# Four pieces of the residual's transposition moved into the norm of the second MLP, and the last modulation vectors streamed through four other buffers

## The chip, the cores and the metric

The kernel runs on one core of a Trainium2 chip. The core has engines that work side by side: TensorE (PE in the profile, with its weight loads as PEld) multiplies matrices, VectorE (DVE) and ScalarE (ACT) work element by element, GpSimd (POOL) does small things, and SyncE (SP) issues the transfers from memory. The metric is the time of one execution on the device in microseconds; lower is better.

## The reference

The reference is a decoder trunk of two layers over 256 positions of 2048 channels. Each layer has a token mixer (a convolution module in layer 0, a Mamba-2 mixer in layer 1) and an MLP with a squared ReLU. Each is preceded by an RMS norm whose result is scaled and shifted by vectors that come from a conditioning vector `c`, and its output is gated by a third such vector and added to the residual `h`:

```python
sc = jax.nn.silu(c)
for i in range(DEPTH):
    mod = (sc @ w_mod[i] + b_mod[i])[:, None, :]
    sh1, sc1, g1, sh2, sc2, g2 = jnp.split(mod, 6, axis=-1)
    ...
    h = h + g1 * mix
    u = rmsnorm(h, norm_mlp_g[i]) * (1 + sc2) + sh2
    h = h + g2 * sq_relu_mlp(u, mlp_w1[i], mlp_w2[i])
return rmsnorm(h, final_norm_g)
```

All is float32. The widths that matter here: `w1` is 2048 x 8192 and `w2` 8192 x 2048; the Mamba mixer's output matrix `wout` is 4096 x 2048.

## The kernel before

**Layout.** The residual is kept as four tiles `h[0]` to `h[3]`, channels on the 128 partitions, four groups of 128 channels and 256 positions to a tile. Weights stream from memory in tiles of 1 MB (`w32`, three buffers, `load_w`). Each tile is split in two halves, and each half in a high part `wh` (a cast on ScalarE, L387) and a low part `wl` (a subtraction on VectorE, L389); both have three buffers. TensorE multiplies the parts and adds up in banks of its accumulator memory. There are eight banks: six of the pool `mm` for the large products and two of the pool `ms` for small ones.

**Order.** The program is traced from top to bottom. A planner then gives every engine a fixed order: what comes first in the program goes first when it is ready, and `high_priority(n)` moves an instruction's rank forward. `issue_after(x)` ties an instruction behind `x` on its engine. Buffers with one tag rotate; a new user waits until the old one's readers are done. Transfers of `stream` (L371) keep the program's order in SyncE's queue.

**Small steps.** Some work is written as generators in `todo`. `block`, the routine for one 512-column block of a matrix, calls `step` (L486) after every second group of products, and each step runs one generator to its next `yield`. `lag(n)` is `n` empty steps.

**Vectors.** The modulation vectors are computed from `w_mod` by `gemv` (L294): a 1 MB piece is fetched (`fetch`, L277) and multiplied with `silu(c)` on VectorE (L317), with the sum over the columns taken along. `pump` starts them in between the products, at rates such as `RATE_OUT` (24 over the 32 tiles of `wout`) and `RATE_LAST` (8 over the twelve tiles of the opening of the second MLP). The attribute `rings` names the tags whose buffers the pieces go to: `("wm",)` in all of layer 1, that is two buffers. The tag `hid` has four buffers of the same size; in the Mamba mixer they hold `out_hl[:4]`, what the first half of `wout` multiplies, and in the MLP the hidden activations.

**Where the change lies.** `mamba` ends with `wout`: four blocks of its first half, then four of its second half (`into_h` adds the gated result to `h`; the very last block is of the kind `single`, L402). Then `mlp(1, ...)` (L1042):

1. It loads the first tile of `w1` and calls `rstd_bcast` (L544). This sums the squares over the channels with TensorE (L575), takes root and reciprocal (L581, L582), forms a diagonal (L549) and broadcasts it with one more product (L554). While the small engines work, `turn` (L285) keeps TensorE occupied with products of constants (`turn_over`, L558): three ahead of the broadcast (`AFTER_SUMS`) and four behind it (`TO_FIRST`, called by `outer`).
2. `outer` (L494) multiplies the first three column blocks of `w1` together, with two `mm` banks for each. For every quarter `g` of the channels `make(g)` (L1054) first scales and shifts that quarter into `u` (`modulate`, L605, with its cast L538), and then three tiles are multiplied.
3. `act` (L1063) squares the positive results and stores them in `hid`.
4. `to_rows` (L1101) is put into `todo`. The second MLP accumulates with positions on the partitions, so the residual is transposed: for each tile `h[b]` and each half `q` of the positions four transposes go to one `ms` bank (L1110), and ScalarE copies the bank into `ht[q]` (L1111), which sits in the two `wm` buffers. Two empty steps follow each of these eight pieces. After that it spreads the gate `G2` along rows by products (L1120, L1124, L1126) and loads the final norm's factor.
5. The last column block of the first quarter of `w1` runs through `block`, then `w2` through `block_t` (L451), and so on for the other quarters.

Of the kernel before, what the change touches and what calls it, by code (L numbers as in the profile page):

```python
# [15 lines left out]
P = 128  # L16
T = 256
D = 2048
# [5 lines left out]
Q = 128  # L24
# [159 lines left out]
def lag(n):  # L184

    for _ in range(n):
        yield


class Trunk:  # L190
    def __init__(self, ctx, nc, tc, a):
        self.nc, self.tc, self.a = nc, tc, a
        pool = lambda n, **kw: ctx.enter_context(tc.tile_pool(name=n, **kw))
        self.one = pool("one", bufs=1)
        self.big = pool("big", bufs=1)
        self.wp = pool("wp", bufs=1)
        self.tp = pool("tp", bufs=2)
        self.mm = pool("mm", bufs=6, space=PSUM)
        self.ms = pool("ms", bufs=2, space=PSUM)
        self.dr = pool("dr", bufs=1, space=DRAM)  # L200
        self.uid = 0
        self.jobs = []
        self.todo = []
        self.ahead = AHEAD
        self.ring, self.rings = 0, ("wm", "hid", "hid")
        self.mod = {}
        self.rows_left = []
        self.held = []
        self.spare = 1
        self.act = None  # L210
        self.side = self.mm, "mm"
        self.prologue()
# [72 lines left out]
    def turn(self, out, n):  # L285

        if self.held:
            key, w = self.held.pop(0)
            with self.tc.issue_after(self.pe):
                self.gemv(*key, w=w)  # L290
        else:
            self.pe = self.turn_over(out, n, self.pe)

    def gemv(self, layer, seg, ct, parts=((0, 4),), w=None):  # L294

        nc = self.nc
        w = self.fetch(layer, seg, ct) if w is None else w
        g, i = divmod(ct, 4)
        m = self.mod_tile(layer, seg, g)
        if (layer, seg, g) in PE_GROUPS:  # L300

            if i == 0:
                while len(self.rows_left) > self.spare:
                    self.columns()
                self.row_sums = self.bank(*self.side)
            for t in range(4):
                kt = 4 * i + t
                self.pe = nc.tensor.matmul(
                    self.row_sums[32 * t:32 * t + 32, :], lhsT=self.scol[:, kt:kt + 1].broadcast_to([P, 32]),
                    rhs=w[:, t * 512:(t + 1) * 512], start=i == 0, stop=i == 3, skip_group_check=True).ins  # L310
            if i == 3:
                row = self.t("t2", [P, 512], bufs=3)
                with self.tc.issue_after(self.act):
                    nc.scalar.copy(out=row, in_=self.row_sums)
                self.rows_left.append([self.row_sums, row, m, layer, seg, g, 0])
            return
        self.sum = nc.vector.scalar_tensor_tensor(out=w, in0=w, scalar=1.0, in1=self.scb, op0=ALU.mult,  # L317
                                                  op1=ALU.mult, accum_out=m[:, i:i + 1]).ins
        for i0, i1 in parts:
            if i + 1 == i1:  # L320
                self.mod_done(layer, seg, g, i0, i1)
# [720 lines left out]
    def mlp(self, layer, ss, pump=None, after=None, first=None):  # L1042
        nc, a = self.nc, self.a
        w = self.load_w(a["w1"][layer, 0][0])
        with self.tc.high_priority(AHEAD_CHAIN):
            half = self.split_half(w, 0, None, self.evac)
            r = self.rstd_bcast(ss, D)
        u = []
        st = {"acc": [None] * 4, "ss": []}
        gate = lambda b: self.mod_tile(layer, G2, b)  # L1050
        self.sq_row = self.t("mom", [P, 2, 4], bufs=1)
        self.part = [None] * 2

        def make(g):  # L1054
            self.need(layer, SC2, SH2, kg=g)
            with self.tc.high_priority(0 if g else AHEAD_CHAIN):
                u.append(self.modulate(r, layer, SC2, SH2, g))
            return u[g]

        for c in range(4):  # L1060
            hid = [None] * 4

            def act(b, j, parts):  # L1063
                if hid[b] is None:
                    self.rings = ("wm",)
                    hid[b] = self.b("hid", [P, 4, 2 * T], F32R)
                s = self.total(parts)
                q = self.t("a", [P, T], bufs=3)
                if len(parts) == 1:
                    nc.scalar.activation(out=q, in_=s, func=AF.Relu)  # L1070
                    s = q
                    nc.vector.tensor_mul(q, q, q)
                else:
                    nc.vector.scalar_tensor_tensor(out=q, in0=s, scalar=0.0, in1=s, op0=ALU.max, op1=ALU.mult)
                self.split_x(hid[b], j, q)

            if c == 0:
                self.outer([a["w1"][layer, b] for b in range(OPEN)], make, act, first or (lambda g: 0),
                           there=[(w, [half])], hi_after=self.sq)
                if layer == 1:  # L1080
                    self.todo.append(self.to_rows())
            for b in range(0 if c else OPEN, 4):
                self.block(a["w1"][layer, 4 * c + b], u, lambda j, parts, b=b: act(b, j, parts), pump=pump)
            if layer == 1:
                for b in range(4):
                    self.block_t(a["w2"][layer, c, b], hid, self.into_rows(b, c == 3), by_half=c == 3 and b == 3)
                continue
            for b in range(4):
                if c == 3:
                    self.need(layer, G2)  # L1090
                if b < 3:
                    ev = self.into_h(st, b, gate, after, acc=False) if c == 3 else None
                    self.block_t(a["w2"][layer, c, b], hid, self.into_turned(st, b, c, ev), pump=pump)
                    continue
                ev = self.into_h(st, b, gate, after) if c == 3 else self.into_acc(st, b, c == 0)
                self.block(a["w2"][layer, c, b], hid, ev, pump=pump, single=c == 3)
        assert not self.todo
        return st["ss"]


    def to_rows(self):  # L1101

        nc = self.nc
        self.need(1, G2)
        self.ht = [self.b("wm", [P, D], bufs=2) for _ in range(2)]
        for b in range(4):
            for q in range(2):
                ps = self.bank(self.ms, "ms")
                for j in range(4):
                    nc.tensor.transpose(ps[:, j * P:(j + 1) * P], self.h[b][:, j, q * Q:(q + 1) * Q], self.ident)  # L1110
                nc.scalar.copy(out=self.ht[q][:, b * 512:(b + 1) * 512], in_=ps)  # L1111
                yield from lag(2)
        self.gate_row, self.fg_row = [], []
        for i in range(2):
            v = self.b("h", [P, 2, 512])
            for k in range(2):
                ps = self.bank(self.ms, "ms")
                m = self.mod_tile(1, G2, 2 * i + k)
                dg = self.t("t2", [P, 4, P], bufs=3)
                nc.vector.tensor_tensor(  # L1120
                    out=dg, in0=self.ident.rearrange("p (o k) -> p o k", o=1).broadcast_to([P, 4, P]),
                    in1=m.rearrange("p (j o) -> p j o", o=1).broadcast_to([P, 4, P]), op=ALU.mult)
                yield from lag(3)
                nc.tensor.matmul(ps, lhsT=self.ones, rhs=dg.rearrange("p j k -> p (j k)"), start=True, stop=True)  # L1124
                yield
                nc.scalar.copy(out=v[:, k, :], in_=ps)  # L1126
                self.gate_row.append(v[:, k, :])
        for i in range(2):
            v = self.b("h", [P, 2, 512])
            src = self.a["fg"][:, i * 1024:(i + 1) * 1024]  # L1130
            nc.scalar.dma_start(out=v.rearrange("p k n -> p (k n)"), in_=src.broadcast_to([P, 1024]))
            self.fg_row += [v[:, 0, :], v[:, 1, :]]
# [39 lines left out]
    def mamba(self, ss):  # L1172
        nc, a = self.nc, self.a
# [74 lines left out]
        while self.todo:  # L1248
            self.step()
        self.need(1, G1)  # L1250
        for b in range(4):
            self.block(a["wout"][1, b], self.out_hl[4:], self.into_h(st, b, gate), pump=pump, single=b == 3)
        self.need(1, SC2, SH2)
# [236 lines left out]
```

## Time and profile before

| | us |
|---|---|
| median of 3 runs | 2538.79 |
| lowest and highest of the runs | 2536.79, 2539.12 |
| the profiled execution | 2537.33 |
| its span (first to last recorded instruction) | 2535.5 |
| mean granted clock of TensorE | 0.999 of full speed |
| norm of the second MLP (last product of `wout` to first product of `w1`) | from 1807.6 to 1812.4 |
| transposes of the residual, 32 instructions in all | from 1810.1 to 1905.9 |
| ScalarE's copies of the transposed residual, 8 | 0.587 each |

How to read it: the page gives the busy time of each engine as a share of the span, and a chain of work that is followed back from the last instruction, so that the engine which set the end has the largest share of it. A row of the timeline has the start, the time it took, the engine, the line and what was written from what, and in brackets the idle time before it with what ended it. `x4` means that four records were merged. Products of float32 operands that are not marked for the fast float32 form appear as two records.

### The profile page before, as it was taken

What the parts mean: (1) busy time and instruction counts of PE and PEld (TensorE: products, weight loads), DVE (VectorE), ACT (ScalarE), POOL (GpSimd) and SP (SyncE); (2) the same over time, 40 slices, a digit from 0 to 9 for tenths busy, and PEclk for the clock granted to TensorE, in tenths of its full rate; (3) what the DMA queues carried; (4) which work ended last, traced back from release to release, by engine and by line L of the source; (5) the groups of instructions that cost most, each with busy time, mean ns of one, the idle gap of its engine ahead of it and who ended that gap; (6) DMA issues with size and microseconds to landing.
All of it is one profiled execution on the core that took longest, in us unless ns stands there. A gap on an engine that the chain in (4) does not pass through costs nothing.

```text
span 2535.5 us, 36834 instructions
## 1 busy us (share of the span) xinstructions
PE 2509.7 (99%) x14596; PEld 2166.1 (85%) x14596; DVE 1937.3 (76%) x2524; ACT 1320.2 (52%) x2026; POOL 145.1 (6%) x201
## 2 busy tenths in 40 slices
PE   9999999999999999999999999999999999999998
PEld 7788799988888888888888888888998888888887
DVE  6799888878878888888787878998875565565565
ACT  2088654544434435457777777744454443443444
POOL 0011000000100000001000000000001101001000
PEclk9999999999999999999999999999999999999999
DMA  9998898788888878856555555688765555555554
GB/s 401 420 351 286 343 347 312 281 332 316 321 309 334 322 307 336 311 201 229 199 190 179 171 189 189 254 322 318 288 249 196 194 188 193 189 190 192 193 189 149
DMA packets 94894, 664.31 MB, mean 262 GB/s; under 512 B 10977, under 2 KB 11105, under 8 KB 16769
## 3 DMA queue, kind: packets, MB, share of 16 engines
q1 hardware_dynamic: 89138, 643.82, 68.6%
q0 software_dynamic: 5152, 16.97, 2.4%
q8 instruction: 114, 1.87, 0.3%
q10 hardware_dynamic: 432, 1.19, 0.1%
q14 instruction: 58, 0.48, 0.0%
HBM read 656.50 MB, written 2.20 MB: 260 GB/s over the span
## 4 chain that ended last, share of the span: by engine, by line
PE 89%; DVE 5%; DMA 3%; ACT 2%; issue 1%; SPq 0%; POOL 0%; DVEq 0%; ACTq 0%; POOLq 0%
PE mm L418 49%; PE mm L402 11%; PE mm L460 8%; PE mm L462 8%; PE mm L461 8%; DMA hid<-wmT 2%; DVE taps L693 2%; ACT taps L675 1%; PE mm L797 1%; DVE hid L317 1%; PE ms L1413 1%; DMA wm<-wmT 1%; DVE wm L317 1%; PE ms L797 0%; DVE taps L687 0%
## 5 line engine op out<-in xcount | busy, mean ns | idle before, releaser
L389 DVE TENSOR_TENSOR wl<-w,wh 128x1024 fp32r<-128x1024 f32 x768 | 940.2, 1229 | 474.1 <-ACT wh L387 469.4
L387 ACT CAST wh<-w 128x1024 fp32r<-128x1024 f32 x768 | 806.4, 1051 | 932.2 <-PE mm L418 480.6
L418 PE MATMUL mm<-u,wh 128*128 128x512 f32 x3136 | 994.6, 398 | 0.0
L418 PEld LDWEIGHTS mm<-u,wl 128*128 128x128 f32 x3136 | 587.9, 188 | 139.9 <-DVE wl L389 1.9
L418 PE MATMUL mm<-u,wl 128*128 128x256 f32 x3136 | 617.3, 278 | 1.4 <-DVE wl L389 1.4
L418 PEld LDWEIGHTS mm<-u,wh 128*128 128x128 f32 x3136 | 479.4, 189 | 7.2 <-issue 4.9
L460 PE MATMUL mm<-wh,hid 128*128 128x512 f32 x896 | 350.7, 391 | 0.0
L462 PE MATMUL mm<-wh,hid 128*128 128x512 f32 x896 | 348.7, 389 | 0.0
L461 PE MATMUL mm<-wl,hid 128*128 128x512 f32 x896 | 348.6, 389 | 0.0
L317 DVE SCALAR_TENSOR_TENSOR wm<-wm,scb 128x2048 f32<-128x2048 f32 x134 | 306.2, 2285 | 13.8 <-DMA wm<-wmT 13.7
L402 PE MATMUL mm<-u,wh 128*128 128x256 f32 x1408 | 253.7, 284 | 0.5 <-ACT u L538 0.3
L402 PEld LDWEIGHTS mm<-u,wh 128*128 128x128 f32 x1408 | 218.3, 192 | 3.5 <-ACT u L538 1.3
L461 PEld LDWEIGHTS mm<-wl,hid 128*128 128x128 f32 x896 | 168.2, 188 | 35.5 <-issue 0.5
L462 PEld LDWEIGHTS mm<-wh,hid 128*128 128x128 f32 x896 | 168.2, 188 | 35.4
L460 PEld LDWEIGHTS mm<-wh,hid 128*128 128x128 f32 x896 | 168.2, 188 | 35.1 <-issue 1.0
L402 PE MATMUL mm<-u,wl 128*128 128x256 f32 x704 | 196.1, 283 | 0.3 <-DVE wl L389 0.2
L418 PE MATMUL mm<-hid,wh 128*128 128x512 f32 x448 | 142.0, 398 | 0.0
L402 PEld LDWEIGHTS mm<-u,wl 128*128 128x128 f32 x704 | 133.7, 192 | 0.7 <-DVE wl L389 0.7
L317 DVE SCALAR_TENSOR_TENSOR hid<-hid,scb 128x2048 f32<-128x2048 f32 x46 | 105.2, 2287 | 20.5 <-DMA hid<-wmT 19.8
L675 ACT ACTIVATE taps<-u,par 128x256 f32<-128x256 f32 x248 | 102.4, 500 | 9.1 <-DVE u L665 5.3
L418 PEld LDWEIGHTS mm<-hid,wl 128*128 128x128 f32 x448 | 84.1, 188 | 19.7
L346 POOL TENSOR_TENSOR mod<-mod,par 128x4 f32<-128x4 f32 x40 | 38.9, 972 | 1062.0 <-DVE wm L317 900.5
(263 smaller groups left out, 2191.5 us busy)
## 6 DMA issues: line engine op xcount, KB each, us to landing
w<-w SPq DMA_DIRECT2D x256, 1024.0 KB, 5.0
wm<-wmT SPq DMA_DIRECT2D x139, 1024.0 KB, 7.3
w<-win SPq DMA_DIRECT2D x80, 1024.0 KB, 4.9
hid<-wmT SPq DMA_DIRECT2D x53, 1024.0 KB, 12.3
w<-wout SPq DMA_DIRECT2D x32, 1024.0 KB, 6.9
w<-pw SPq DMA_DIRECT2D x27, 1024.0 KB, 6.0
w<-open SPq DMA_DIRECT2D x16, 1024.0 KB, 14.0
acc<-ac_d POOLq DMA_DIRECT2D x16, 512.0 KB, 8.7
```

Source lines behind the costliest of these rows:

```text
L317: self.sum = nc.vector.scalar_tensor_tensor(out=w, in0=w, scalar=1.0, in1=self.scb, op0=ALU.mult, op1=ALU.mult, accum_out=m[:, i:i + 1]).ins
L346: nc.gpsimd.tensor_tensor(out=m, in0=m, in1=b, op=ALU.add)
L387: nc.scalar.copy(out=wh, in_=w[:, s, :])
L389: nc.vector.tensor_tensor(out=wl, in0=w[:, s, :], in1=wh.bitcast(F32), op=ALU.subtract)
L402: self.pe = self.nc.tensor.matmul(out, lhsT=lhsT, rhs=rhs, skip_group_check=True, **kw).ins
L418: self.pe = self.nc.tensor.matmul(out, lhsT=lhsT, rhs=rhs, start=start and not lows, stop=stop and bool(lows), skip_group_check=True).ins
L460: mm(banks[q], lhsT=hi, rhs=wh[:, k, :], start=t == 0, stop=False)
L461: mm(banks[q], lhsT=hi, rhs=wl[:, k, :], start=False, stop=False)
L462: mm(banks[q], lhsT=lo, rhs=wh[:, k, :], start=False, stop=t == NT - 1)
L675: st["tap"] = nc.scalar.activation(out=p4[:, q, :], in_=vp[:, k + q:k + q + T], func=AF.Identity, scale=self.col("w_dw", ct * TAPS + k + q ...
L693: nc.vector.tensor_add(wide, wide, products(four("wl"), k))
L797: self.pe = nc.tensor.matmul(o, lhsT=w[:, i, j * P:(j + 1) * P], rhs=u[g][:, t, :], start=ct == 0 and j < 2, stop=ct == NT - 1, skip_group ...
```

## The change

The change does three things.

- The first four of the eight pieces (tiles `h[0]` and `h[1]`, both halves of the positions) are transposed within `turn`, in place of the products of constants: two pieces where there were three such products, two where there were four. They go to banks of the pool `mm`. ScalarE copies them into `ht` in `make(0)`, tied behind the last cast of the first quarter of `u`.
- `to_rows` keeps the other four pieces, in `ms` banks, and ties each behind the product that was traced last.
- From the second half of `wout` on, the pieces of `w_mod` go to the four `hid` buffers; `ht` takes the two `wm` buffers at the beginning of the second MLP, and `act` sets the ring to `wm` in layer 0 alone.

```diff
+        self.useful, self.pieces = [], []
...
+        elif self.useful:
+            for piece in self.useful[:2]:
+                self.turn_rows(*piece)
+            self.useful = self.useful[2:]
         else:
             self.pe = self.turn_over(out, n, self.pe)
+
+    def turn_rows(self, b, q):
+
+        ps = self.bank(self.mm, "mm")
+        with self.tc.issue_after(self.pe):
+            for j in range(4):
+                self.pe = self.nc.tensor.transpose(ps[:, j * P:(j + 1) * P], self.h[b][:, j, q * Q:(q + 1) * Q],
+                                                   self.ident).ins
+        self.pieces.append((b, q, ps))
...
     def mlp(self, layer, ss, pump=None, after=None, first=None):
         nc, a = self.nc, self.a
         w = self.load_w(a["w1"][layer, 0][0])
+        if layer == 1:
+            self.ht = [self.b("wm", [P, D], bufs=2) for _ in range(2)]
+            self.useful = [(b, q) for b in range(2) for q in range(2)]
...
                 u.append(self.modulate(r, layer, SC2, SH2, g))
+            if layer == 1 and g == 0:
+                for b, q, ps in self.pieces:
+                    with self.tc.issue_after(self.hi):
+                        nc.scalar.copy(out=self.ht[q][:, b * 512:(b + 1) * 512], in_=ps)
             return u[g]
...
                 if hid[b] is None:
-                    self.rings = ("wm",)
+                    if layer == 0:
+                        self.rings = ("wm",)
...
         self.need(1, G2)
-        self.ht = [self.b("wm", [P, D], bufs=2) for _ in range(2)]
-        for b in range(4):
+        for b in range(2, 4):
             for q in range(2):
                 ps = self.bank(self.ms, "ms")
-                for j in range(4):
-                    nc.tensor.transpose(ps[:, j * P:(j + 1) * P], self.h[b][:, j, q * Q:(q + 1) * Q], self.ident)
+                with self.tc.issue_after(self.pe):
+                    for j in range(4):
+                        nc.tensor.transpose(ps[:, j * P:(j + 1) * P], self.h[b][:, j, q * Q:(q + 1) * Q], self.ident)
                 nc.scalar.copy(out=self.ht[q][:, b * 512:(b + 1) * 512], in_=ps)
                 yield from lag(2)
...
         self.need(1, G1)
+        self.rings = ("hid",)
         for b in range(4):
             self.block(a["wout"][1, b], self.out_hl[4:], self.into_h(st, b, gate), pump=pump, single=b == 3)
```

## The prediction

> **What bounds the kernel now.** I read three views in this order: the page's engine totals, its chain of work that ended last, and then the busy time by stretches around the place of the change.
>
> ```profile
> PE 2509.7 (99%) x14596; PEld 2166.1 (85%) x14596; DVE 1937.3 (76%) x2524; ACT 1320.2 (52%) x2026; POOL 145.1 (6%) x201
> ...
> PE 89%; DVE 5%; DMA 3%; ACT 2%; issue 1%; SPq 0%; POOL 0%; DVEq 0%; ACTq 0%; POOLq 0%
> ```
>
> TensorE is busy for 99% of the span and carries 89% of the chain. A shorter TensorE programme shortens the kernel; anything else counts only if TensorE waits for it. The stretches (columns: PE, PEld, DVE, ACT, POOL busy, granted clock, DMA share, GB/s) tell where it waits:
>
> ```profile
> 1760.00:1800.00 40.00, 40.00 (x270) 36.77 (x270) 38.22 (x50) 17.73 (x23) 1.12 (x1) 1.00 0.83 314
> ...
> 1807.60:1812.40 4.80, 4.54 (x38) 4.16 (x36) 3.08 (x7) 3.40 (x7) 0.00 (x0) 1.00 0.49 205
> ...
> 1865.00:1882.00 17.00, 17.00 (x143) 16.96 (x142) 14.28 (x23) 10.91 (x23) 1.11 (x1) 1.00 0.60 214
> 1882.00:1910.00 28.00, 28.00 (x169) 24.65 (x168) 16.56 (x26) 18.03 (x31) 0.00 (x0) 1.00 0.54 184
> ```
>
> Before and behind the norm of the second MLP TensorE is busy all the time: 40.00 of 40 us, 17.00 of 17, 28.00 of 28. Only the 4.8 us of the norm are different: there TensorE is busy too, but with filler. The chain in order of time shows this stretch and the transposes later on:
>
> ```profile
> 1784.60 23.17 PE mm L402 x192
> 1807.76 1.68 PE ms L575 x16
> 1809.44 0.78 PE ms L562 x6
> 1810.22 0.44 PE ms L1110 x4
> 1810.65 0.60 PE ms L554 x2
> 1811.28 0.49 DVE nrm L610
> 1811.86 0.52 ACT u L538
> 1812.42 69.42 PE mm L402 x576
> 1881.84 4.18 PE mm L418 x24
> 1886.02 0.44 PE ms L1110 x4
> 1886.46 2.80 PE mm L418 x16
> 1889.26 0.44 PE ms L1110 x4
> ...
> 1905.46 0.44 PE ms L1110 x4
> ```
>
> L562 is the filler (products of constants), L1110 the residual's transposes, four to a piece. There are eight pieces. One, of b=0 and q=0, already runs inside the norm, at 1810.22, because nothing held it back; the other seven stand between the products of the last block of w1, from 1886.02 to 1905.46. Each of those takes 0.44 us of a TensorE that never pauses: 1889.26 - 1886.02 = 3.24 us from piece to piece, of which 2.80 are the sixteen products.
>
> **The change part by part.** First the transposes. The change puts sixteen transposes (four pieces) into the norm and leaves four pieces in the last block of w1, now tied behind the product traced before them, so that none of them can slip into the norm any more. In the body there were seven pieces and there are four: 3 x 0.44 = 1.32 us less for TensorE. It is three and not four, since the eighth was free already.
>
> Second, whether the norm has room. The filler goes: three products ahead of the broadcast of the norm (six records, float32 takes two each) and four behind it (eight records).
>
> ```profile
> 1809.30 0.91 PE L562 MATMUL ms<-scb,ones 128*128 128x128 f32 x6
> 1810.05 0.60 PE L1110 MATMUL ms<-ident,h 128*128 128x128 f32 x4
> 1811.08 1.05 PE L562 MATMUL mm<-scb,ones 128*128 128x128 f32 x8
> 1812.42 0.91 PE L402 MATMUL mm<-u,wh 128*128 128x256 f32 x5 [0.28 <-ACT u L538]
> ...
> L1110 PE MATMUL ms<-ident,h x32: 272/273/274, 1810.1 to 1905.6; 128*128 128x128 f32 x32
> ...
> 1810.07 0.42 DVE L549 TENSOR_TENSOR diag<-ident,rcol 128x256 f32<-128x256 f32 x1
> ```
>
> Four transposes take 0.60 us, of which the last one's own duration is 0.273: one starts (0.60 - 0.273) / 3 = 0.11 us behind the other. Eight take 8 x 0.11 = 0.88 us of issue. Ahead of the broadcast they run from 1809.30 to 1810.18, and the broadcast cannot start before VectorE's diagonal at 1810.07 + 0.42 = 1810.49: 0.3 us to spare. Behind it they run from 1811.08 to 1811.96, and the first product of w1 waits for ScalarE's u until 1812.42: 0.46 us to spare. So the sixteen transposes cost nothing, and the removed filler gains nothing; the cover is the chain of square root, reciprocal, diagonal, scaling and cast. If that cover were gone, they would cost 4 x 0.44 = 1.76 us. What is late next is the same chain: the norm still ends at 1812.42. At most the 0.28 us that TensorE sits idle there could be won; I take 0.
>
> Third, the banks. The four pieces stay in four of the six mm banks until ScalarE has copied them, and w1's opening takes all six: two each for its three column blocks. This is a new wait. The residual's last update out of a bank and ScalarE's copies and casts:
>
> ```profile
> 1807.80 0.48 DVE L989 SCALAR_TENSOR_TENSOR h<-mm,mod,h 128x256 f32<-128x256 f32 x1 [0.23 <-PE mm L402]
> ...
> L1111 ACT COPY wm<-ms x8: 579/587/589, 1865.4 to 1905.9; 128x512 f32<-128x512 f32 x8
> ...
> 1813.71 0.91 ACT L538 ACTIVATE u<-nrm,mod 128x256 fp32r<-128x256 f32 x2 [0.94 <-DVE nrm L610]
> 1815.81 1.05 ACT L387 CAST wh<-w 128x1024 fp32r<-128x1024 f32 x1 [1.19 <-PE mm L402]
> 1818.80 1.06 ACT L387 CAST wh<-w 128x1024 fp32r<-128x1024 f32 x1 [1.94 <-PE mm L402]
> 1821.32 1.05 ACT L387 CAST wh<-w 128x1024 fp32r<-128x1024 f32 x1 [1.46 <-PE mm L402]
> ```
>
> All banks are free at 1808.28, so the pieces need not wait for one. A half of a w1 tile is 24 products, 24 x 69.42 / 576 = 2.89 us, so the second column block starts at 1812.42 + 2 x 2.89 = 1818.20 and wants two banks, the third at 1823.98. The copies come behind the last cast of the first quarter of u, which ends at 1814.62. ScalarE then idles 1.19 us, and 1.94 us behind the next cast: two copies of 0.587 end at 1815.79, the other two by 1818.04. Both are in time. Queued behind a copy is the cast of the next half tile; VectorE waits for it and then TensorE. The cast of 1815.81 is the fourth half's, wanted at 1821.09; with its 1.05 us and the low part on VectorE (1.22, row below) it is ready at 1818.08. A copy ahead of it takes 0.6 of 3.0 us. Cost 0; bounds 0 and, where the copies come late, 2.83 us a column block (the second rival).
>
> Fourth, the vectors' weights. From the second half of wout on, twenty of them (twelve, then eight in w1's opening) go to the four hid buffers in place of the two wm buffers.
>
> ```profile
> SPq L373 <- DVE wl L389: 65.2, 16, 12.0
> SPq L373 <- DVE wm L317: 33.2, 7, 8.8
> ...
> DVE wm L317 <- DMA wm<-wmT: 0.9, 1, 0.9
> PE mm L402 <- ACT u L538: 0.3, 1, 0.3
> ...
> 1706.13 0.43 SPq L373 DMA_DIRECT2D wm<-wmT  x1
> ...
> L317 DVE SCALAR_TENSOR_TENSOR wm<-wm,scb x27: 2281/2285/2294, 1659.4 to 1870.3; 128x2048 f32<-128x2048 f32 x27
> L389 DVE TENSOR_TENSOR wl<-w,wh 128x1024 fp32r<-128x1024 f32 x35 | 42.6, 1223 | 15.5 <-ACT wh L387 15.1
> ```
>
> SyncE's queue waits 33.2 us for a wm buffer, ahead of weight tiles; two more buffers shorten that. But nobody waits for those tiles: in w1's opening TensorE waits 0.3 us in all, for u, and VectorE 0.9 us for one vector. So the shorter wait gains 0. The new wait: the first such load needs the first hid buffer, which wout's first half reads. Its last block begins 5 x 22.4 us before 1807.6, at 1695.6 (a block is 16 x 8 products; 23.17 us for 192 shorter ones here, and much the same for the others), and is done with that buffer a quarter later, at some 1701, ahead of the load at 1706.13; the second to fourth buffer follow in steps of 5.6 us. Behind it in the queue stand the weight tiles of wout, for which the casts wait; nothing to pay. The opening's results want hid from about 1869 on, and only two vectors are then outstanding for four buffers. VectorE's work is the same, 2.285 us each. Bounds: 0, and what a reordering on VectorE may cost (third rival).
>
> Fifth, the gate rows and the two loads of the final norm's row come eight steps, some 11 us, earlier, since four pieces with their pauses are gone from the queue of small steps. Their products and copies are as many as before, in a stretch with TensorE busy 28.00 of 28 us: 0.
>
> Sum: 1.32 us. The profiled execution took 2537.33 us around a span of 2535.5; it becomes 2536.0. The median of the runs is 1.46 us above the profiled one, so I expect 2538.79 - 1.32 = 2537.5, -0.05%. That is below 0.2% (5.1 us), about what a measurement of this kernel can tell from no change.
>
> [...] The granted clock is 1.00 in every row of the stretches above, and the rows of the kernel's end show how it falls.
>
> ```profile
> 2520.00:2530.00 10.00, 6.61 (x30) 5.13 (x28) 5.67 (x10) 3.82 (x8) 0.00 (x0) 0.98 0.27 105
> 2530.00:2535.00 5.00, 0.00 (x0) 0.00 (x0) 0.53 (x2) 0.52 (x1) 0.00 (x0) 0.50 0.53 210
> ```
>
> TensorE stops at 2526.61 there; a mean of 0.98 is 0.4 us at half clock within 10 us, so the clock fell at 2529.6, 3.0 us later. In the norm the stretches that would hold transposes alone, 1809.44 to 1810.65 and 1811.25 to 1812.42, last 1.2 us each. [...]
>
> **The rivals.**
>
> *Half of the pieces miss the norm* (the change doesn't do what it says). The opening's six banks are asked for in the program ahead of the third and fourth piece. If the planner gives out banks in that order, those two wait until ScalarE has emptied one and then run in the body: 7 - 6 = 1 piece won, 0.44 us: 2538.3. For it: six banks, ten takers. Against it: the product that uses a bank is later than the transposes, and a bank need not be taken before its first use.
>
> *Slower: the copies come late on ScalarE.* Place: the second column block of the opening. It decides at 1818.20, when its two banks must be empty. The cast of 1821.32 needs a buffer that this column block frees, so the copies can be no later than just ahead of it: behind the cast that ends at 1819.86, plus 2 x 0.587 = 1821.03, a stall of 2.83 us; once more for the third block at worst. Net -1.32 + 2.83 = +1.51: 2540.3; twice, 2543.1. For it: the casts are put ahead by priority, the copies are not. Against: 1.19 + 1.94 us of idle ScalarE before that point.
>
> *Slower: VectorE's order.* With data earlier, the planner may put two vectors ahead of a low part: 2 x 2.285 against the 3.0 us of reserve, 1.6 us lost: 2539.1. Against: low parts have the higher priority.
>
> *The clock falls in the norm.* If transposes do not hold the clock and it stays down about as long as it took to fall, 3.0 us at half speed lose 1.5 us: 2537.5 + 1.5 = 2539.0. Against: sums until 1809.44 and the broadcast of 0.60 us lie between, and each stretch is 1.2 us, not 3.0.
>
> **How the numbers follow.** The forecast has 0.74, the missed half 0.10, the late copies 0.07, the clock 0.05, VectorE's order 0.04. All lie within 5.1 us of 2538.79; only late copies twice over together with a high run, or several small losses, get past it: slower 0.04, faster 0.02 (1.32 + 0.28 us is all that can be won here, the rest would be drift), same 0.94. The runs before span 2536.79 to 2539.12. The low end is the lowest of them less 1.32 and 0.28, and 0.6 more, a quarter of that spread, as three runs do not show all of it: 2534.6. The high end is the highest run with one late pair, 2539.12 + 1.51 = 2540.6.
>
> **What would show it.** Four pieces of transposes between 1809 and 1812 and none of the constants' products there; the first product of w1 again some 4.8 us behind the last of wout; four pieces in the last block of w1, and the first product of w2 1.3 us earlier against that first one. Right for the banks: TensorE without a wait at the second and third column block. Wrong: a wait of TensorE for a copy there, transposes found within the opening, a granted clock below 1.00 behind the norm, or TensorE waiting for a low part in wout's second half.

## The result and the profile after

| | before | changed kernel |
|---|---|---|
| median, us | 2537.52 | 2541.06 |
| lowest and highest, us | 2535.84, 2539.12 | 2540.47, 2543.49 |
| runs | 22 | 22 |
| span of the profiled execution, us | 2535.5 | 2539.5 |

The changed kernel is slower by 3.5 us: ratio 1.0015, 95% interval 1.001 to 1.0021. The forecast was 2537.5, with a range that ended at 2540.6. The difference is below the 0.2% that the prediction took for no change, but with 22 runs a side it is plain (the interval does not reach 1), it has the other sign, and the time lies above the range.

The lines of the changed kernel have moved by 14 or 22 (L402 is now L416, L387 is L401, L1070 is L1092, L1110 is L1132); its own L387 is the line of `stream`, which was L373. New are L304, the transposes in the norm, and L1078, their copies. The page's totals hardly show anything:

```profile
span 2539.5 us, 36800 instructions
...
PE 2510.4 (99%) x14582; PEld 2166.6 (85%) x14582; DVE 1937.5 (76%) x2524; ACT 1321.3 (52%) x2026; POOL 143.6 (6%) x201
```

TensorE's busy time is 0.7 us longer, and the span 4.0. So TensorE waits somewhere. Of the 4.0 us, 1.0 lies ahead of the norm (its first product starts at 1808.57 instead of 1807.60), where this execution lost 1.7 us to a lower clock (0.83 in the 10 us from 1120 on, against 1.00 before; last section); 3.0 lie behind. The norm comes first, since the change was made there. TensorE's timeline of the changed kernel (start, time, engine, line, what, and in brackets the idle time and what ended it):

```profile
1808.57 0.50 PE L589 MATMUL ms<-ones,ssum 128*128 128x1 f32 x4
...
1810.27 1.07 PE L304 MATMUL mm<-ident,h 128*128 128x128 f32 x8
1811.51 0.70 PE L568 MATMUL ms<-diag,ones 128*128 128x256 f32 x2 [0.17 <-DVE diag L563]
1812.04 1.04 PE L304 MATMUL mm<-ident,h 128*128 128x128 f32 x8
1813.38 0.90 PE L416 MATMUL mm<-u,wh 128*128 128x256 f32 x3 [0.30 <-ACT u L552]
```

All sixteen transposes lie between the sums and the first product of w1, and no product of constants is left. From the first sum to the first product of w1 it takes 1813.38 - 1808.57 = 4.81 us; before it was 1812.42 - 1807.60 = 4.82. The norm is as forecast. The waits of TensorE behind it, first those from 1812 to 1885, then those from there on (engine, tile and line, waited for what: total, times, longest; us):

```profile
PE mm L416 <- ACT wh L401: 2.0, 1, 2.0
...
PE mm L416 <- DVE wl L403: 0.5, 1, 0.5
```

```profile
PE mm L432 <- ACT wh L401: 0.9, 1, 0.9
```

Before, the only row was the 0.3 us for u, which is still there. New is that TensorE waits for a cast of ScalarE (2.0), for the low part that VectorE makes of it (0.5), and for one more cast (0.9). The chain of the changed kernel says where (start, us, what):

```profile
1813.90 63.39 PE mm L416 x526
...
1878.30 0.95 ACT wh L401
...
1880.55 4.12 PE mm L416 x32
...
1886.04 0.95 ACT wh L401
```

Before, one row of 69.42 us of products stood here, without a break. Now it breaks twice, at the end of w1's opening, and each time the chain goes through a cast of a weight tile (L401), ahead of which it has a result (L1092, and its own cast into `hid`, L549; left out here). TensorE's timeline gives the price:

```profile
1877.00 0.28 PE L416 MATMUL mm<-u,wl 128*128 128x256 f32 x1
1879.29 0.74 PE L416 MATMUL mm<-u,wh 128*128 128x256 f32 x4 [2.01 <-ACT wh L401]
1880.55 0.39 PE L416 MATMUL mm<-u,wl 128*128 128x256 f32 x1 [0.52 <-DVE wl L403]
1880.78 0.40 PE L416 MATMUL mm<-u,wh 128*128 128x256 f32 x2
...
1885.81 0.28 PE L416 MATMUL mm<-u,wl 128*128 128x256 f32 x1
1887.03 1.66 PE L432 MATMUL mm<-u,wh 128*128 128x512 f32 x6 [0.94 <-ACT wh L401]
```

Products follow one another by 0.12 us (63.39 us for 526). From 1877.00 to 1880.78 there are six, 0.72 us' worth, in 3.78 us: 3.06 lost. From 1885.81 to 1887.03 there is one: 1.10 lost. Together 4.2 us, against which stand the 1.3 us that the transposes give back: net 2.9.

ScalarE's timeline shows why the cast was late. Before:

```profile
1867.41 1.05 ACT L387 CAST wh<-w 128x1024 fp32r<-128x1024 f32 x1 [1.40 <-PE mm L402]
1868.92 0.66 ACT L1070 ACTIVATE a<-mm 128x256 f32<-128x256 f32 x2 [0.46 <-PE mm L402]
...
1870.40 1.05 ACT L387 CAST wh<-w 128x1024 fp32r<-128x1024 f32 x1
...
1873.17 1.05 ACT L387 CAST wh<-w 128x1024 fp32r<-128x1024 f32 x1 [1.14 <-PE mm L402]
```

And the changed kernel:

```profile
1868.56 1.05 ACT L401 CAST wh<-w 128x1024 fp32r<-128x1024 f32 x1 [1.83 <-PE mm L416]
1870.12 0.66 ACT L1092 ACTIVATE a<-mm 128x256 f32<-128x256 f32 x2 [0.51 <-PE mm L416]
...
1872.80 0.74 ACT L549 CAST hid<-a 128x256 fp32r<-128x256 f32 x2 [0.27 <-DVE a L1094]
1875.94 0.66 ACT L1092 ACTIVATE a<-mm 128x256 f32<-128x256 f32 x2 [2.39 <-PE mm L416]
...
1878.20 1.99 ACT L401 CAST wh<-w 128x1024 fp32r<-128x1024 f32 x2
```

L387 and L401 are the casts of weights, L1070 and L1092 the results. Before, a cast of weights comes about every 2.9 us, with results between. After the change none starts between 1868.56 and 1878.20. The casts had been 2.88 us apart (1865.68 and 1868.56), so the next could have come at some 1871.4. Instead four results of the column block just finished run first, and then the first result of the next column block stands at the head of ScalarE's queue: 2.39 us of idle, until TensorE has finished the sum that it reads. The cast that TensorE will soon need stands behind it, and in those 2.39 us, from 1873.55 to 1875.94, ScalarE's timeline has no record: nothing overtakes the result.

So the planner, which writes every engine's order beforehand, put three results ahead of the two casts of the opening's last tile, and results of that last tile ahead of the next block's first casts. The transfer of the weight tile was not late. SyncE's queue of the changed kernel, with the load of the seventh vector of the opening and then that of the opening's last tile:

```profile
1855.29 0.43 SPq L387 DMA_DIRECT2D hid<-wmT  x1
1859.43 0.33 SPq L387 DMA_DIRECT2D w<-w  x1
```

And before:

```profile
1858.22 0.33 SPq L373 DMA_DIRECT2D w<-w  x1
```

The opening's last tile was asked for at 1859.43, some 12 us ahead of 1871.4. Counted from the first product of w1 that is 46.05 us, and before it was 45.80. And the cast, when its turn came at 1878.20, did not wait for a transfer: its row has no idle time ahead of it. What made the cast late is its place in the planned order.

### The profile page after: what moved, and what is told of

Read it like the earlier page. It is cut to its first block, busy times and chain, and to the rows that moved or that the text cites. A ratio compares the mean times of both kernels' runs of the same rounds, so it can differ in the third digit from the quotient of the medians.

```text
span 2539.5 us, 36800 instructions
## 1 busy us (share of the span) xinstructions
PE 2510.4 (99%) x14582; PEld 2166.6 (85%) x14582; DVE 1937.5 (76%) x2524; ACT 1321.3 (52%) x2026; POOL 143.6 (6%) x201
## 4 chain that ended last, share of the span: by engine, by line
PE 89%; DVE 5%; DMA 3%; ACT 2%; issue 1%; SPq 0%; POOL 0%; DVEq 0%; ACTq 0%; POOLq 0%
PE mm L432 49%; PE mm L416 11%; PE mm L475 8%; PE mm L476 8%; PE mm L474 8%; DMA hid<-wmT 2%; DVE taps L707 2%; ACT taps L689 1%; PE mm L811 1%; DVE hid L331 1%; PE ms L1436 1%; DMA wm<-wmT 1%; DVE wm L331 0%; PE ms L811 0%; DVE taps L701 0%
## 5 line engine op out<-in xcount | busy, mean ns | idle before, releaser
L401 ACT CAST wh<-w 128x1024 fp32r<-128x1024 f32 x768 | 807.3, 1052 | 934.0 <-PE mm L432 478.7
L331 DVE SCALAR_TENSOR_TENSOR wm<-wm,scb 128x2048 f32<-128x2048 f32 x114 | 260.6, 2286 | 10.6 <-DMA wm<-wmT 10.6
L416 PE MATMUL mm<-u,wh 128*128 128x256 f32 x1408 | 254.1, 284 | 2.5 <-ACT wh L401 2.0
L416 PEld LDWEIGHTS mm<-u,wh 128*128 128x128 f32 x1408 | 218.3, 192 | 6.0 <-ACT wh L401 3.1
L416 PE MATMUL mm<-u,wl 128*128 128x256 f32 x704 | 196.2, 283 | 0.8 <-DVE wl L403 0.7
L331 DVE SCALAR_TENSOR_TENSOR hid<-hid,scb 128x2048 f32<-128x2048 f32 x66 | 151.1, 2289 | 19.2 <-DMA hid<-wmT 19.1
L416 PEld LDWEIGHTS mm<-u,wl 128*128 128x128 f32 x704 | 133.7, 192 | 1.4 <-DVE wl L403 1.4
```

Source lines behind the costliest of these rows:

```text
L401: nc.scalar.copy(out=wh, in_=w[:, s, :])
L416: self.pe = self.nc.tensor.matmul(out, lhsT=lhsT, rhs=rhs, skip_group_check=True, **kw).ins
```

## The experiments

Two theories stood against each other. **A**: the vectors' move to `hid` changes ScalarE's fixed order, and the stall is all of the loss. The seventh vector of the opening is traced behind the first results of the opening. It asks for a `hid` buffer (its claim), and the first result tile has just asked for one. The next vector load and the weight tile behind it stand in SyncE's queue behind that claim; the planner takes them to be late and plans the casts late. **B**: the transposes, their copies or the banks (or the clock in the norm) cause it. The stretch ahead of the norm differs by a few us between profiles, in part because the clock falls there in some and not in others (last section), so I also compare the time from the first product of the sums to the end of the span. It leaves out all that lies ahead of the norm. Each row is one profile; how much this time scatters between executions of one kernel was not measured.

| kernel | first sum at | span | from there to the end | against before |
|---|---|---|---|---|
| before | 1807.60 | 2535.5 | 727.9 | |
| changed | 1808.57 | 2539.5 | 730.9 | +3.0 |
| e1, vectors alone | 1809.50 | 2539.7 | 730.2 | +2.3 |
| e2, transposes alone | 1807.32 | 2534.1 | 726.8 | -1.1 |
| e3, all vectors ahead of the results | 1808.03 | 2534.7 | 726.7 | -1.2 |
| e4, one vector behind a result | 1806.67 | 2539.8 | 733.1 | +5.2 |
| e5, casts put first | 1811.07 | 2537.8 | 726.7 | -1.2 |
| e6, e3 and an untied fifth piece | 1807.30 | 2533.5 | 726.2 | -1.7 |
| e7, no filler | 1810.48 | 2539.8 | 729.3 | +1.4 |

**e1: the vectors alone.** The kernel before, with the vectors' weights in `hid`; the transposes, the constants and `ht` stay.

```diff
                 if hid[b] is None:
-                    self.rings = ("wm",)
+                    if layer == 0:
+                        self.rings = ("wm",)
...
         self.need(1, G1)
+        self.rings = ("hid",)
         for b in range(4):
```

> The kernel before with one part of the change: the vectors' weights go to the four hid buffers from the second half of wout on; all transposes stay where they were. Theory A (the order of claims on hid): the load of the seventh vector of w1's opening claims its hid buffer in the program behind the first result tile, so the planner expects that load, and the weight tile queued behind it, late, and puts ScalarE's casts of the opening's last tile behind results; TensorE then stalls some 4.5 us near the opening's end as in the changed kernel: +4 us against the kernel before (+3 to +5.5). Rival B (the transposes in the norm and their copies on ScalarE are what costs): within 0.5 us of the kernel before, no stall of TensorE near the opening's end.

Measured: 2539.96 us (median of 11) against 2537.69, +2.3; ratio 1.0007, interval 0.9998 to 1.0016. ScalarE waits as in the changed kernel. ScalarE's timeline of e1:

```profile
1876.64 0.66 ACT L1071 ACTIVATE a<-mm 128x256 f32<-128x256 f32 x2 [2.39 <-PE mm L402]
...
1880.11 1.99 ACT L387 CAST wh<-w 128x1024 fp32r<-128x1024 f32 x2
```

The same 2.39 us at the head of the queue, with two casts late behind it, and no transpose was moved. The loss is less than the 4 us expected because something useful fell into the hole. TensorE's timeline of e1:

```profile
1878.94 1.15 PE L1111 MATMUL ms<-ident,h 128*128 128x128 f32 x8 [0.41 <-ACT wm L1112]
...
1881.21 0.74 PE L402 MATMUL mm<-u,wh 128*128 128x256 f32 x4 [0.29 <-ACT wh L387]
```

In this kernel the pieces are not tied, so two of them run at 1878.94, and about two more just ahead and behind, while TensorE has nothing else to do. In the changed kernel they are tied behind later products and cannot. The interval of the medians takes in no change by itself; the 2.39 us and the late casts are the evidence for A.

**e2: the transposes alone.** The changed kernel with the vectors left in `wm`. Since `ht` cannot have the `wm` buffers then, its rows go to four tiles of another tag with half the length.

```diff
-            self.ht = [self.b("wm", [P, D], bufs=2) for _ in range(2)]
+            self.ht = [[self.b("acc", [P, 1024], bufs=5) for _ in range(2)] for _ in range(2)]
...
-                    if layer == 0:
-                        self.rings = ("wm",)
+                    self.rings = ("wm",)
...
-        self.rings = ("hid",)
```

> The changed kernel with the vectors left in the two wm buffers; the transposed residual goes to four acc buffers (two of 1024 columns for each half of the positions) in their place. Theory A: no stall near the opening's end, and three pieces of transposes (0.44 us each) less in the body: -1.3 us against the kernel before (-0.5 to -2). Rival B: +3.5 us as in the changed kernel (+2.5 to +4.5).

Measured: 2536.93 us (11 runs) against 2537.69; ratio 0.9995, interval 0.9986 to 1.0004. The medians alone cannot tell it from no change; the time from the norm on is 1.1 us shorter. The chain of e2 has its unbroken row of products again:

```profile
1812.65 69.14 PE mm L416 x574
```

From 1660 to 1960 TensorE waits only 0.3 us for u and 0.2 for the diagonal. B falls: transposes, banks and copies cost nothing, and the time from the norm on agrees with the 1.32 us of the forecast.

**e3: the last two vectors ahead of the results.** Everything of the change stays. Only the rate at which the eight vectors are started in the opening is altered, so that all eight are traced before the first result asks for `hid`.

```diff
-RATE_LAST = spread(8, 12)
+RATE_LAST = [0, 1, 1, 0, 1, 1, 0, 1, 1, 2, 0, 0]
```

`spread(8, 12)` is 0, 1, 1 four times over; the zero-one-one of the last quarter becomes two-zero-zero.

> The changed kernel, but the last two vectors of the opening are both started at the first tile of the last quarter (one and two tiles sooner), so that their claims on hid stand in the program ahead of the first result tile's. Theory A: the planner has no reason to expect the last tile late, the casts stand ahead of the results, no stall: -1.3 us against the kernel before (-0.5 to -2). Rival B: +3.5 us, since transposes, copies and buffers are those of the changed kernel. Rival C (the four hid buffers cost by themselves, in wout or by where they lie): +3.5 to +4.8 us.

Measured: 2536.75 us (11 runs) against 2537.69; ratio 0.9992, interval 0.9984 to 1.0001; 1.2 us shorter from the norm on. The chain of e3:

```profile
1813.37 69.14 PE mm L416 x574
```

No break. The vectors still use `hid`, so it is not the buffers themselves that cost, but that claims of vectors stand behind claims of results. It takes both: in e2 the last two vectors are traced as late as in the changed kernel, but on `wm`, and nothing stalls. The interval of e3 ends at 1.0001, that of the changed kernel begins at 1.001.

**e4: one vector behind a result.** As e3, but one of the eight stays behind the first two column blocks' results.

```diff
-RATE_LAST = spread(8, 12)
+RATE_LAST = [0, 1, 1, 0, 1, 1, 0, 1, 1, 1, 0, 1]
```

> The changed kernel, but of the last two vectors only the eighth stays behind a result tile's claim (at the last tile); the seventh is started at the first tile of the last quarter, ahead of it. Theory A: the last tile's casts are in their place, and only those of the following block stand behind results; of the changed kernel's two stalls (some 2.7 and 1.8 us) the second is left: -1.3 + 1.8 = +0.5 us against the kernel before (-0.3 to +2). Rivals B and C: +3.5 us.

Measured: 2542.52 us against 2537.69; ratio 1.0018, interval 1.0009 to 1.0027. I missed the size by far, 4.8 in place of 0.5. TensorE's waits in e4 from 1660 to 1960:

```profile
PE mm L432 <- ACT wh L401: 3.8, 1, 3.8
PE mm L432 <- DVE wl L403: 0.5, 1, 0.5
```

The first break is gone, as expected: no row has a cast ahead of L416. The second has grown from 0.9 to 3.8 + 0.5. ScalarE's timeline of e4:

```profile
1883.56 0.38 ACT L1092 ACTIVATE a<-mm 128x256 f32<-128x256 f32 x1 [1.86 <-DVE hid L550]
1883.84 1.98 ACT L401 CAST wh<-w 128x1024 fp32r<-128x1024 f32 x2
```

Now all four results of the opening's last column block stand ahead of both casts of the next block. I had taken the two stalls for separate, with one vector behind each; they are not, and one vector behind a result is enough. Behind the longer pause the clock also fell in this profile. One stretch of e4 (bounds, length, busy time of PE, PEld, DVE, ACT, POOL with instructions, granted clock, DMA share, GB/s):

```profile
1885.00:1890.00 5.00, 4.47 (x17) 3.66 (x18) 4.08 (x5) 2.96 (x5) 0.00 (x0) 0.66 0.33 98
```

The clock was 0.50 from 1887 to 1889 there, so 0.66 over 5 us is 3.4 us at half speed, 1.7 us of TensorE's work. 3.8 + 0.5 + 1.7 = 6.0, less 1.2 (e3) is 4.8, which is what the medians show (5.2 from the norm on); that the clock fell in the other ten runs too is not shown.

**e5: ScalarE's order alone.** The changed kernel with its vectors at their own rate, but the opening's last tile is loaded and split in the program ahead of the products of the tile before, and the results of that tile before are tied behind the casts.

```diff
+                tied = self.tied and g == 3 and b == 1
+                if tied:
+                    w = self.load_w(srcs[2][g])
...
+                        kept.append(self.split_w(w))
...
-                            for q in (j - 2, j):
-                                evac(b, q, [banks[b][j - 2][:, (q // 2) * T:(q // 2 + 1) * T]])
+                            with self.tc.issue_after(self.cast) if tied else nullcontext():
+                                for q in (j - 2, j):
+                                    evac(b, q, [banks[b][j - 2][:, (q // 2) * T:(q // 2 + 1) * T]])
```

> The changed kernel with its buffers and the seventh vector's claim as they are (behind the first result tile), but the opening's last tile is loaded and split in the program ahead of the products of the tile before it, and ScalarE's results of that tile are tied behind the last tile's two casts; the eighth vector's load moves ahead of those results with it. Theory A in its second half (the weight tile itself lands early enough, and only ScalarE's fixed order makes TensorE wait): no stall of over 1 us at the opening's last tile, and about the time of the kernel without the clash: -1.3 us against the kernel before (-1.8 to +0.5). Rival D (the tile itself comes late, or VectorE's late vectors hold up the low parts, so that the order on ScalarE follows a real lateness): the stall stays, +2.5 us or more.

Measured: 2536.02 us (11 runs) against 2538.22; ratio 0.9993, interval 0.9984 to 1.0002; 1.2 us shorter from the norm on. ScalarE's timeline of e5:

```profile
1875.95 1.99 ACT L402 CAST wh<-w 128x1024 fp32r<-128x1024 f32 x2
1878.44 0.66 ACT L1105 ACTIVATE a<-mm 128x256 f32<-128x256 f32 x2 [0.49 <-PE mm L417]
```

The two casts now run where the changed kernel's ScalarE sat idle, and the result that waits for TensorE comes behind them. The same stretch of TensorE is full in e5:

```profile
1870.00:1880.00 10.00, 10.00 (x86) 10.00 (x85) 8.07 (x14) 6.49 (x14) 0.00 (x0) 1.00 0.55 197
```

So ScalarE's order is the cost; with it put right, the stall is gone while a vector still claims a `hid` buffer behind the results. One reservation: the eighth vector's load moved ahead together with the tile, so not only ScalarE's order was touched.

**e6: a fifth piece in the norm.** e3, and the four pieces that remain are no longer tied behind a product.

```diff
-                with self.tc.issue_after(self.pe):
+                with nullcontext():
```

> The kernel with the last two vectors ahead of the first result tile, and the four remaining pieces no longer tied behind the product traced before them. Theory A: the planner puts a fifth piece into the norm, where 0.3 and 0.46 us were to spare, so that three pieces are left in the body: -1.3 - 0.44 = -1.7 us against the kernel before (-0.9 to -2.4). If the norm has no room for it, the first product of the opening comes up to 0.44 us later and the time stays at -1.3.

Measured: 2535.76 us (11 runs) against 2538.22; ratio 0.9993, interval 0.9984 to 1.0002; 1.7 us shorter from the norm on, the size expected. TensorE's timeline of e6:

```profile
1811.65 0.38 PE L1132 MATMUL ms<-ident,h 128*128 128x128 f32 x2
...
1812.46 0.38 PE L1132 MATMUL ms<-ident,h 128*128 128x128 f32 x2
```

Half of a fifth piece fits into the 0.3 us in which TensorE waits for u; the other half comes behind the first two products of w1, which the expectation did not have. It costs nothing there either: the opening's products end 1881.77 - 1807.30 = 74.47 us behind the first sum, in e3 1882.51 - 1808.03 = 74.48, and three pieces are left in the body. This kernel has the lowest median of the study, though its interval still takes in no change; against the changed kernel it gains 4.7 us from the norm on.

**e7: no filler at all.** The kernel before without the products of constants in the norm of the second MLP. It leaves out no part of what is computed.

```diff
         else:
-            self.pe = self.turn_over(out, n, self.pe)
+            if not self.bare:
+                self.pe = self.turn_over(out, n, self.pe)
...
+        self.bare = layer == 1
```

> The kernel before without the products of constants in the norm of the second MLP; the planner may put transposes there in their place. If neither those products nor transposes are needed for the clock: granted clock 1.00 behind the norm, the norm 4.8 us as before, and the kernel before's time within 0.5 us. If the clock falls when TensorE has only the sums, the broadcast and a few transposes to do: a clock below 1.00 in the first stretch of the opening and +1.5 to +2 us.

Measured: 2539.08 us (10 runs) against 2538.22; ratio 1.0003, interval 0.9994 to 1.0012; 1.4 us longer from the norm on. The norm in TensorE's timeline of e7, where only the broadcast and one piece of transposes are left between the sums and w1:

```profile
1810.48 0.50 PE L577 MATMUL ms<-ones,ssum 128*128 128x1 f32 x4
...
1815.30 1.44 PE L404 MATMUL mm<-u,wh 128*128 128x256 f32 x5 [0.74 <-ACT u L540]
```

The norm itself takes 1815.30 - 1810.48 = 4.82 us as before, so the constants do not shorten it. What happens without them shows in the stretches of e7:

```profile
1815.00:1818.00 3.00, 2.70 (x12) 2.70 (x13) 2.75 (x6) 1.56 (x4) 0.00 (x0) 0.53 0.00 0
1818.00:1822.00 4.00, 4.00 (x33) 4.00 (x32) 2.83 (x5) 1.05 (x1) 0.00 (x0) 0.92 0.70 240
```

The clock fell to half (0.50, last section). 0.47 x 3 + 0.08 x 4 = 1.7 us of TensorE's work were lost; from the norm to the end this execution is 1.4 longer, and the medians differ by 0.9, with an interval that takes in no change. The fall was seen in this one profile; how often it comes in e7 is not known. The changed kernel's stretches, with sixteen transposes in the norm, show none of it:

```profile
1813.40:1818.00 4.60, 4.58 (x36) 4.38 (x37) 4.60 (x8) 3.42 (x7) 0.00 (x0) 1.00 0.19 30
1818.00:1830.00 12.00, 12.00 (x103) 12.00 (x102) 11.35 (x14) 6.18 (x9) 0.00 (x0) 1.00 0.89 339
```

## Why the prediction was wrong

**The first step, three pieces less for 1.32 us, was right.** Where the stall is absent, the time from the norm on is 1.1 (e2), 1.2 (e3) and 1.2 us (e5) shorter.

**The second step, room in the norm, was right.** 4.81 us in place of 4.82, all sixteen transposes inside, with 0.17 us of idle ahead of the broadcast (0.3 forecast) and 0.30 behind it (0.46 forecast). The forecast counted the starts alone, 0.88 us for eight transposes; with the last one's own time they take 1.07 and 1.04.

**The third step, banks and copies, was right.** The changed kernel's ScalarE:

```profile
1815.49 1.05 ACT L1078 COPY wm<-mm 128x512 f32<-128x512 f32 x2
...
1817.73 1.06 ACT L1078 COPY wm<-mm 128x512 f32<-128x512 f32 x2
```

Two copies, a cast (left out), two copies, done at 1818.79; the second column block begins at 1813.38 + 5.78 = 1819.16, and TensorE has no wait there. That refutes the rivals of the missed half and of the late copies.

**The fourth step, the vectors' weights at no cost, failed.** Its reason was that "the opening's results want hid from about 1869 on, and only two vectors are then outstanding for four buffers". That counts buffers, and on the chip it held: the seventh vector's load was issued at 1855.29, long before the first result at 1870.12. What matters is the order of the claims: two of the vectors claim a `hid` buffer behind a claim by a result. Before, the vectors' claims were on `wm`, the results' on `hid`, and neither could stand behind the other. Now they stand in one row, and the planner's order on ScalarE changed. The step gave only "what a reordering on VectorE may cost" as the bound, and its rival priced VectorE with 1.6 us; the reordering was on ScalarE, an engine that this step did not touch, and cost TensorE 4.2 us, where the step had put 0. The view that would have shown the risk is ScalarE's timeline from 1867 on, which the prediction did not read: casts and results alternate there, a cast every 2.9 us, and a result waits for the end of a column block, so a single cast that slips behind it stops TensorE. The rival on VectorE's order itself did not come true: no row has two vectors ahead of a low part that TensorE waits for, only low parts behind late casts.

**The fifth step, gate rows earlier, was right as far as it shows**: e2, e3 and e5 contain it and have no wait.

**The rival of the clock** did not come true either. That transposes do not hold the clock was its assumption; no run had shown that, and none here does. The granted clock stays 1.00 through and behind the norm with sixteen float32 transposes, in this profile and in those of e2 to e6, and falls in e7, which lacks the filler and has four. In none of the six profiles with the transposes did the clock fall in the norm, nor in the two with the constants (before and e1). That it falls without either rests on e7's single profile. In e7 the fall lost 1.7 us in 3.4 us; the prediction's estimate had 1.5 in 3.0.

Shown is that the vectors' move makes the stall (e1 has it, e2 does not), that it hangs on vectors traced behind results (e3, e4), and that the order of casts and results carries it (e5, with the reservation given there). The intervals of e2, e3 and e5 end at 1.0004 or below, under that of the changed kernel. That the planner takes the weight tile to be late because of the claim ahead of it is argued from these orders; its own reckoning of times was not looked into.

## What to carry to other kernels

Moving transfers to another tag of buffers does not only change how many buffers there are, but also whose claims stand in one row; where a planner fixes every engine's order beforehand, an order far away can change, on an engine that the edit does not touch. So count not only buffers but go through the claims on the tag in the order of the program, and have every transfer claim ahead of a result that becomes ready late; here one line, the starting rate, turned +3.5 us into about -1 (e3, whose own interval takes in no change). When the forecast gain is about 1 us, put a price on every engine's order around the place where the two users of a tag meet, not only on the engine that does the moved work.

## What the runs showed of the hardware

**The clock fell for 3.4 us in e7 and in e4.** Stretches of e7, half a microsecond each; those left out between them have 0.50:

```profile
1815.00:1815.50 0.50, 0.20 (x1) 0.20 (x2) 0.26 (x2) 0.50 (x2) 0.00 (x0) 0.71 0.00 0
...
1818.50:1819.00 0.50, 0.50 (x5) 0.50 (x5) 0.50 (x2) 0.00 (x0) 0.00 (x0) 0.88 0.12 33
```

The shares put the fall at 1815.21 (0.29 us at half speed make 0.71) and the rise at 1818.62: 3.4 us, as the 3.4 us at half speed in e4. In e7 it came just ahead of TensorE's next product at 1815.30; in e4 it came only after TensorE was at work again (the pause ends at 1884.93, the clock is 1.00 from 1880 to 1886 and 0.77 in the half microsecond behind). The price was the same 1.7 us for a pause of 1.10 + 0.74 us with short work between and for one of 3.8 us. The changed kernel's 2.01 + 0.52 us went without (1.00 in every stretch from 1870 to 1910). Ahead of 2520 us the nine profiles together show eleven such falls, nine of them ahead of the norm, and each lost 1.6 to 1.7 us (granted clock 0.83 or 0.84 in the 10 us that hold it).

**The clock fell at the same pauses in one execution and not in another.** At the beginning of the Mamba mixer, which the change does not touch, TensorE waits 1.4, 1.2, 0.4 and 0.4 us in eight of the nine profiles (in e5, whose clock had fallen just ahead, 1.4, 1.0 and 0.4). One stretch there, in the profile before and in that of the changed kernel:

```profile
1124.00:1126.00 2.00, 1.68 (x12) 1.59 (x13) 1.98 (x6) 1.38 (x2) 0.00 (x0) 1.00 0.80 336
```

```profile
1124.00:1126.00 2.00, 2.00 (x10) 1.81 (x10) 1.30 (x4) 1.15 (x2) 0.00 (x0) 0.56 0.58 234
```

The clock fell there (0.56 in this stretch of the changed kernel, 1.00 before) in the changed kernel, e1, e3, e5 and e6; it did not in the kernel before, e2, e4 and e7. So the length of the pauses alone does not decide it here; what else does was not tested. Two things follow for this study: times of single executions carry steps of 1.6 to 1.7 us here that have nothing to do with the edit, in e5's profile four ahead of the norm; and a fall in one profile, as in e7 or e4, shows that the clock can fall at such a pause (0.53 and 0.66 there), not that it does so every time.
